# A hybrid encoder block on one core: MLA queries made feature-major, per head pair, with rotary tables turned during the mixer and latents normed for all tokens at once

## Chip, cores and metric

The kernel runs on 1 core of one Trainium2 chip. The metric is the device time of one execution in microseconds (us). The kernel before took 987.62 us, the median of 3 runs (987.09 to 988.03).

## The reference, cut to what matters

One layer on 512 tokens of width 1024: an RMS norm, one input projection that feeds a Mamba-2 (SSD) mixer and a multi-head latent attention (MLA), an output projection of both, a memory cross-attention, a convolution FFN and a last norm. The change touches the MLA queries:

```
q_lat, kv_lat, k_rope = split(u, [384, 640])
q = (rmsnorm(q_lat) @ w_q_up).reshape(b, s, 16, 64 + 32)
q_nope, q_rope = split(q, [64])
kv = (rmsnorm(kv_lat) @ w_kv_up).reshape(b, s, 16, 64 + 64)
q_rope = [t1 * cos - t2 * sin, t1 * sin + t2 * cos]   # t1, t2: halves of 16; k_rope likewise
sc = (q_nope . k_nope + q_rope . k_rope) * 96 ** -0.5, block-causal mask, softmax, times v
```

## The kernel before, in words

Every product runs in three matmuls (`mm3`, L101 to L105): both operands are split into a high and a low part (`split`, L92: a ScalarE copy makes the high part, a VectorE subtraction the low one), and hi*hi, hi*lo and lo*hi add up in one PSUM bank. Weights come as pages of 512 KB over SyncE's DMA queue (`wload`, three raw buffers `wr`), and are split into `wh` and `wl` (four buffers each); while `pool_helps` is set, GpSimd does half of the low part (L158). The PSUM banks are three `acc`, two `tr` (transposes), two `s` (scores), one `pv`.

The order that is written down is a priority: the compiler's list scheduler places each instruction on its engine by a simulated timeline, and fills with later ready work. SyncE and GpSimd issue their DMAs in order.

The mixer walks 16 steps (4 groups of heads by 4 chunks of 128 tokens), each with `ssd_a`, `ssd_b`, `ssd_d` for a chunk. Groups 0 to 2 mix in the projections of the next group; in the last group a string per chunk (`PLAN`, L35) says what goes between: `l` the late units that project the latents (`late_unit`, L665), `i` their setup, `q0` to `q3` and `k0` to `k3` norm and transpose the query and key latents of one 128-token tile (`lat_norm`, L616), `p` a part of the output projection (`out_part`), `U` the query up-projection of heads 0 to 3, `s` and `S` the setup of query and key operands. `lat_norm` takes a sum of squares on ScalarE, a power on GpSimd, a scaling on VectorE, three or two transposes and as many splits into `LT` (the latents feature-major, five tiles of 128 features by 512 tokens).

`q_up` (L712) runs once per four heads: for each of four token tiles nine matmuls of 384 columns (tokens on partitions), a copy to `qrow`, and four GpSimd operations for the rotation. `prep` (L762) then transposes each head's queries back, four 128-token pieces of 96 features, into an `acc` bank, and splits them into one of two operands `qt`. `prep(i + 2)` is called while head i is finished, after the scores of head i + 1. The attention loop (L905) overlaps scores of head i + 1, transposed probabilities and `pv` of head i, and fill units (the rest of the output projection, memory keys and values) at fixed places.

Of the kernel before, what the change touches and what calls it, by code (L numbers as in the profile page):

```python
# [7 lines left out]
F32 = mybir.dt.float32  # L8
# [26 lines left out]
PLAN = ('z z z z d a l l b', 'l l d a i q0 k0 p1 q1 b p1 q2 k1 p1 q3 k2', 'p1 d a k3 p1 b p1', 'p1 d U p2 b p3 s S')  # L35


def shape_constants():
# [4 lines left out]
    m = np.zeros((NT, 2, T), np.float32)  # L43
    for j in range(NT):
        m[j, 0, j * P:j * P + 64] = 1.0
        m[j, 1, j * P + 64:(j + 1) * P] = MASK_NEG
# [16 lines left out]
def tile_block(ctx, tc, x, mem, positions, norm_mix_w, w_in, ssd_conv_w, ssd_conv_b, ssd_dt_bias,  # L63
# [62 lines left out]
    def k4(shape, name, dt=F32):  # L126
        return base.tile(list(shape), dt, name=name, tag="k4", bufs=13)
# [105 lines left out]
    cenT = base.tile([P, NT, SSD_H], F32, name="cenT")  # L233
    acT = dram.tile([NT, SSD_H, P], F32, name="acT")
# [370 lines left out]
    def lat_init():  # L605
# [4 lines left out]
        box["ln"] = qkl[:, QR + KVR:]  # L610
        nc.vector.tensor_scalar(box["qw"], box["qw"], float(QH) ** -0.5, None, ALU.mult)
        x4 = k4([P, 4, 256], "xo")
        xo.extend(x4[:, i] for i in range(3))
        box["lnk"] = [gw[0], x4[:, 3]]

    def lat_norm(t, o, n, w, l0, l1, ln):  # L616
        ss = small([P, 1], "ssl", 2)
        src = lat[:, t, SSD_H + o:SSD_H + o + n]
        nc.scalar.activation(ln, src, AF.Square, accum_out=ss)
        rs = rstd_of(ss, n, "l")  # L620
        nc.vector.scalar_tensor_tensor(ln, src, rs, w, ALU.mult, ALU.mult)
        ps = tr_bank().rearrange("p (k t) -> p k t", k=4)
        for k in range(l0, l1):
            transpose(ps[:, k - l0], ln[:, tsl(k - l0)])
        for k in range(l0, l1):
            split(LT[k][:, 0, tsl(t)], LT[k][:, 1, tsl(t)], ps[:, k - l0])

    def lat_q(t):
        lat_norm(t, 0, QR, box["qw"], 0, 3, box["ln"])

    def lat_kv(t):
        lat_norm(t, QR, KVR, box["kvw"], 3, 5, box["lnk"][t % 2])
        kr = lat[:, t, SSD_H + QR + KVR:]
        tmp = small([P, ROPE], "krt", 1)
        nc.vector.tensor_tensor(tmp[:, 0:H2], kr[:, H2:], sinb[:, t, 0:H2], ALU.mult)
        nc.vector.tensor_tensor(tmp[:, H2:], kr[:, 0:H2], sinb[:, t, H2:], ALU.mult)
        nc.vector.tensor_tensor(kr, kr, cosb[:, t], ALU.mult)
# [589 lines left out]
```

## Time and profile before

| what | before |
|---|---|
| runs shown, median (range) | 987.62 us (987.09 to 988.03) |
| the profiled execution | 987.27 us |
| its span in the profile | 985.5 us |
| its mean granted TensorE clock | 0.994 |
| instructions | 14980 |

The span is the time from the first to the last instruction of the profile; 1.8 us of the profiled execution lie around it. A window row gives, for a stretch of the span, each engine's busy time with its count of instructions, the granted TensorE clock as a share of full speed, and what the DMA engines did. Matmuls are pipelined, so a matmul's own duration is longer than the step from one start to the next; the steps are read from start times.

### The profile page before, as it was taken

What the parts mean: (1) busy time and instruction counts of PE and PEld (TensorE: products, weight loads), DVE (VectorE), ACT (ScalarE), POOL (GpSimd) and SP (SyncE); (2) the same over time, 40 slices, a digit from 0 to 9 for tenths busy, and PEclk for the clock granted to TensorE, in tenths of its full rate; (3) what the DMA queues carried; (4) which work ended last, traced back from release to release, by engine and by line L of the source; (5) the groups of instructions that cost most, each with busy time, mean ns of one, the idle gap of its engine ahead of it and who ended that gap; (6) DMA issues with size and microseconds to landing.
All of it is one profiled execution on the core that took longest, in us unless ns stands there. A gap on an engine that the chain in (4) does not pass through costs nothing.

```text
span 985.5 us, 14980 instructions
## 1 busy us (share of the span) xinstructions
PE 965.7 (98%) x5385; PEld 843.0 (86%) x5385; DVE 662.1 (67%) x1210; ACT 523.4 (53%) x1078; POOL 279.6 (28%) x360
## 2 busy tenths in 40 slices
PE   8999999999999999999999999999999999999997
PEld 6889998898899999988888888888888888888886
DVE  5989999868779786773654435766667666722553
ACT  5677776655477677753544434444444444321442
POOL 2016547656653547452443222000000000000000
PEclk9999999999999999999999999999999999999999
DMA  7653432315423336242241120433223322332462
GB/s 242 208 175 95 116 108 77 97 49 179 155 78 103 113 113 233 86 155 80 86 150 65 65 86 22 128 107 107 86 87 108 105 85 93 113 116 97 156 223 80
DMA packets 90306, 114.07 MB, mean 116 GB/s; under 512 B 5799, under 2 KB 70119, under 8 KB 89848
## 3 DMA queue, kind: packets, MB, share of 16 engines
q1 hardware_dynamic: 88536, 106.78, 34.0%
q0 software_dynamic: 1696, 6.33, 2.1%
q8 instruction: 43, 0.70, 0.3%
q14 instruction: 31, 0.25, 0.1%
HBM read 104.67 MB, written 8.42 MB: 115 GB/s over the span
## 4 chain that ended last, share of the span: by engine, by line
PE 82%; DVE 7%; DMA 3%; ACT 3%; POOL 2%; issue 2%; SPq 0%; POOLq 0%; ACTq 0%; DVEq 0%
PE acc L103 22%; PE acc L105 22%; PE acc L104 22%; PE tr L119 3%; PE s L103 3%; PE s L105 3%; PE s L104 3%; PE pv L811 2%; DMA aE<-acT 2%; DVE wl L157 1%; ACT aE L544 1%; PE acc L119 1%; DVE cu L434 1%; DMA wr<-in_w_in_dram 1%; POOL xdD L550 1%
## 5 line engine op out<-in xcount | busy, mean ns | idle before, releaser
L103 PE MATMUL acc<-Ah,wh 128*128 128x512 f32 (+1 forms) x560 | 215.5, 385 | 0.2 <-ACT Ah L94 0.2
L104 PE MATMUL acc<-Al,wh 128*128 128x512 f32 (+1 forms) x560 | 215.4, 385 | 0.2 <-DVE Al L95 0.2
L105 PE MATMUL acc<-Ah,wl 128*128 128x512 f32 (+1 forms) x560 | 215.0, 384 | 0.0
L95 DVE TENSOR_TENSOR wl<-wr,wh 128x1024 fp32r<-128x1024 f32 (+1 forms) x99 | 120.0, 1213 | 101.6 <-ACT wh L94 100.9
L94 ACT CAST wh<-wr 128x1024 fp32r<-128x1024 f32 (+1 forms) x99 | 102.0, 1031 | 133.5 <-PE acc L104 63.7
L158 POOL TENSOR_TENSOR wl<-wr,wh 128x512 fp32r<-128x512 f32 (+2 forms) x64 | 103.5, 1625 | 86.2 <-ACT wh L156 79.8
L142 POOL TENSOR_TENSOR rs<-ms,neg_half 128x1 f32<-128x1 f32 x18 | 10.8, 600 | 409.5 <-DVE ms L140 397.9
L104 PEld LDWEIGHTS acc<-Al,wh 128*128 128x128 f32 x560 | 105.3, 188 | 20.3 <-DVE Al L95 0.5
L105 PEld LDWEIGHTS acc<-Ah,wl 128*128 128x128 f32 x560 | 105.3, 188 | 20.2
L103 PEld LDWEIGHTS acc<-Ah,wh 128*128 128x128 f32 x560 | 105.2, 188 | 20.0 <-ACT Ah L94 0.5
L156 ACT CAST wh<-wr 128x1024 fp32r<-128x1024 f32 (+2 forms) x64 | 65.4, 1029 | 40.1 <-PE s L105 10.7
L1121 DVE SCALAR_TENSOR_TENSOR cbuf<-acc,fcw,cbuf 128x511 f32<-128x511 f32 (+1 forms) x88 | 65.6, 747 | 26.6 <-ACT cbuf L1119 25.1
L157 DVE TENSOR_TENSOR wl<-wr,wh 128x512 fp32r<-128x512 f32 (+2 forms) x64 | 59.3, 932 | 35.7 <-ACT wh L156 34.7
L103 PE MATMUL acc<-wh,Ah 128*128 128x256 f32 (+2 forms) x240 | 77.2, 323 | 1.0 <-ACT Ah L94 1.0
L105 PE MATMUL acc<-wh,Al 128*128 128x256 f32 (+2 forms) x240 | 76.2, 319 | 0.0
L104 PE MATMUL acc<-wl,Ah 128*128 128x256 f32 (+2 forms) x240 | 75.9, 318 | 0.0
L795 POOL TENSOR_SCALAR p<-p,ri 128x128 f32<-128x128 f32 (+1 forms) x64 | 34.5, 542 | 71.7 <-DVE ri L794 71.1
L103 PEld LDWEIGHTS acc<-wh,Ah 128*128 128x128 f32 x240 | 46.1, 192 | 4.2 <-ACT Ah L94 1.4
L105 PEld LDWEIGHTS acc<-wh,Al 128*128 128x128 f32 x240 | 46.1, 192 | 2.6 <-DVE Al L95 0.3
L104 PEld LDWEIGHTS acc<-wl,Ah 128*128 128x128 f32 x240 | 46.2, 192 | 2.3
L1119 ACT ACTIVATE cbuf<-acc,fcb,fcw 128x512 f32<-128x512 f32 x44 | 34.3, 779 | 24.0 <-PE acc L105 24.0
L104 PE MATMUL acc<-wl,act 128*128 128x512 f32 (+1 forms) x112 | 40.5, 363 | 0.0
(370 smaller groups left out, 2349.3 us busy)
## 6 DMA issues: line engine op xcount, KB each, us to landing
wr<-in_w_ffn_up_dram SPq DMA_DIRECT2D x44, 512.0 KB, 3.5
wr<-in_w_ffn_down_dram SPq DMA_DIRECT2D x33, 512.0 KB, 3.3
wr<-in_w_in_dram SPq DMA_DIRECT2D x26, 512.0 KB, 3.9
wr<-in_w_out_dram SPq DMA_DIRECT2D x16, 512.0 KB, 3.5
aE<-acT POOLq DMA_DIRECT2D x16, 256.0 KB, 3.5
wr<-in_w_mem_k_dram SPq DMA_DIRECT2D x8, 512.0 KB, 4.5
wr<-in_w_mem_v_dram SPq DMA_DIRECT2D x8, 512.0 KB, 3.4
wr<-in_w_mem_q_dram SPq DMA_DIRECT2D x8, 512.0 KB, 3.6
```

The source lines that it names most:

```text
L94: first = nc.scalar.copy(hi, src)
L95: nc.vector.tensor_tensor(lo, src, f32(hi), ALU.subtract)
L103: nc.tensor.matmul(acc, lhsT=lh, rhs=rh, start=first, stop=False)
L104: nc.tensor.matmul(acc, lhsT=lh, rhs=rl, start=False, stop=False)
L105: nc.tensor.matmul(acc, lhsT=ll, rhs=rh, start=False, stop=last)
L119: nc.tensor.transpose(dst, src, ident[:n, :n])
L156: nc.scalar.copy(hi, raw)
L157: nc.vector.tensor_tensor(lo[:, 0:a // 2], raw[:, 0:a // 2], f32(hi[:, 0:a // 2]), ALU.subtract)
L158: nc.gpsimd.tensor_tensor(lo[:, a // 2:], raw[:, a // 2:], f32(hi[:, a // 2:]), ALU.subtract)
L795: nc.gpsimd.tensor_scalar(p_, p_, ri, 1.0, ALU.mult, ALU.mult)
L1119: nc.scalar.activation(u, acc, AF.Identity, scale=fcw[:, 2, m:m + 1], bias=fcb[:, m:m + 1])
L1121: nc.vector.scalar_tensor_tensor(u[:, s:], acc[:, :T - s], fcw[:, 2 - s, m:m + 1], u[:, s:], ALU.mult, ALU.add)
```

## The change

Queries are made with features on partitions; no head is transposed. `q_rope` runs twice (heads 0 to 7, heads 8 to 15): it loads the rotary columns of eight heads, projects the two halves into two banks of 128 rows (8 heads by 16) by 512 tokens, rotates them against tables `csT` whose rows are frequencies, and keeps both halves in `rq`, split. `q_pair` makes the 64 plain features of two heads in one bank, splits them into two of three operands, and copies the heads' rotary rows from `rq` with DMAs on SyncE's queue, two per head. `prep` of an odd head makes the next pair. `rope_tables` builds `csT` after chunk 2 of group 1, with GpSimd copies, eight transposes and two ScalarE copies. `late_unit` takes the sums of squares; `lat_norm` norms all four token tiles with one power; `lat_T` turns one of five feature blocks for all tokens, with one split. The plan string moves accordingly (and has one output part less), the mask rows arrive with their zeros in one DMA per operand, the pool of 4 KB tiles grows from 13 to 14, and the GpSimd DMA scratch is set to 4096 bytes.

```diff
-PLAN = ('z z z z d a l l b', 'l l d a i q0 k0 p1 q1 b p1 q2 k1 p1 q3 k2', 'p1 d a k3 p1 b p1', 'p1 d U p2 b p3 s S')
+PLAN = ('z z z z d a l l b', 'l l d a i n b p1 t0 p1 t1 t2', 'p1 d a t3 p1 t4 b p1', 'p1 d U p2 b p3 s S')
...
+    def lat_norm():
+        rs = small([P, 2 * NT], "lrs", 1)
+        for i, n in enumerate((QR, KVR)):
+            h = slice(i * NT, (i + 1) * NT)
+            nc.vector.tensor_scalar(lss[:, h], lss[:, h], 1.0 / n, EPS, ALU.mult, ALU.add)
+        nc.gpsimd.tensor_tensor(rs, lss, neg_half.broadcast_to([P, 2 * NT]), ALU.pow)
+        for t in range(NT):
+            for i, (o, n, w) in enumerate(((SSD_H, QR, "qw"), (SSD_H + QR, KVR, "kvw"))):
+                v = lat[:, t, o:o + n]
+                nc.vector.scalar_tensor_tensor(v, v, rs[:, i * NT + t:i * NT + t + 1], box[w], ALU.mult, ALU.mult)
...
+    def lat_T(k):
+        ps = tr_bank()
+        for t in range(NT):
+            transpose(ps[:, tsl(t)], lat[:, t, SSD_H + P * k:SSD_H + P * (k + 1)])
+        split(LT[k][:, 0], LT[k][:, 1], ps)
...
+    def rope_tables():
+        for i, tab in enumerate((cosb, sinb)):
+            ps = tr_bank()
+            for t in range(NT):
+                r = small([P, P], "csr", 2)
+                nc.gpsimd.tensor_copy(r.rearrange("p (h c) -> p h c", c=H2),
+                                      tab[:, t, H2:].unsqueeze(1).broadcast_to([P, 8, H2]))
+                transpose(ps[:, tsl(t)], r)
+            nc.scalar.copy(csT[:, i], ps)
...
         nc.scalar.copy(lat[:, t, 256:], acc)
+        for i, (o, m) in enumerate(((SSD_H, QR), (SSD_H + QR, KVR))):
+            nc.scalar.activation(acc[:, 0:m], lat[:, t, o:o + m], AF.Square, accum_out=lss[:, i * NT + t:i * NT + t + 1])
...
-    def q_up(q4):
...
+    def q_rope(g):
+        raw = base.tile([P, 3, 8, ROPE], F32, name="wr", tag="wr", bufs=3)
+        for k in range(3):
+            nc.sync.dma_start(raw[:, k], mla_w_q_up[0][tsl(k), :].rearrange("p (h c) -> p h c", h=MLA_H)[
+                :, 8 * g:8 * g + 8, NOPE:])
...
+        for k in range(3):
+            hv, lv = (a[:, k].rearrange("p s h c -> p h s c") for a in (hi, lo))
+            split(hv, lv, raw[:, k].rearrange("p h (s c) -> p h s c", s=2))
+        acc = []
+        for s in range(2):
+            acc.append(acc_bank())
             for k in range(3):
+                w = [a[:, k, s].rearrange("p h c -> p (h c)") for a in (hi, lo)]
+                mm3(acc[s], w, (LT[k][:, 0], LT[k][:, 1]), k == 0, k == 2)
+        for s in range(2):
+            a, b = f32(rq[s][:, 0]), f32(rq[s][:, 1])
+            nc.vector.tensor_tensor(b, acc[s], csT[:, 0], ALU.mult)
+            nc.vector.tensor_tensor(a, acc[1 - s], csT[:, 1], ALU.mult)
+            nc.gpsimd.tensor_tensor(b, b, a, ALU.add if s else ALU.subtract)
+            nc.scalar.copy(rq[s][:, 0], b)
+            nc.vector.tensor_tensor(rq[s][:, 1], b, f32(rq[s][:, 0]), ALU.subtract)
+
+    def q_pair(pr):
+        raw = base.tile([P, 3, 2, NOPE], F32, name="wr", tag="wr", bufs=3)
+        for k in range(3):
+            nc.sync.dma_start(raw[:, k], mla_w_q_up[0][tsl(k), :].rearrange("p (h c) -> p h c", h=MLA_H)[
+                :, 2 * pr:2 * pr + 2, 0:NOPE])
...
+        split(hi, lo, raw.rearrange("p k h c -> p k (h c)"))
+        acc = acc_bank()
+        for k in range(3):
+            mm3(acc, (hi[:, k], lo[:, k]), (LT[k][:, 0], LT[k][:, 1]), k == 0, k == 2)
+        for e in range(2):
+            q = qts[(2 * pr + e) % 3]
+            split(q[0:NOPE, 0], q[0:NOPE, 1], acc[e * NOPE:(e + 1) * NOPE])
+            r = H2 * (2 * pr % 8 + e)
+            for s in range(2):
+                nc.sync.dma_start(f32(q[NOPE + H2 * s:NOPE + H2 * (s + 1)]), f32(rq[s][r:r + H2]))
...
-        ps = acc_bank()
-        for t in range(NT):
-            transpose(ps[0:QH, tsl(t)], st["q"][t][:, h % 4])
-        split(qts[h % 2][0:QH, 0], qts[h % 2][0:QH, 1], ps[0:QH])
+        elif h + 1 < MLA_H:
+            q_pair((h + 1) // 2)
...
+            if (g, c) == (1, 2):
+                rope_tables()
...
+    q_pair(0)
     prep(0)
...
-        if i % 4 == 1 and i + 3 < MLA_H:
-            q_up((i + 3) // 4)
+        if i == 3:
+            q_rope(1)
```

## Rows read from the trace of the kernel before

**Rows 1.** The page: busy time of each engine, share, instructions

```profile
PE 965.7 (98%) x5385; PEld 843.0 (86%) x5385; DVE 662.1 (67%) x1210; ACT 523.4 (53%) x1078; POOL 279.6 (28%) x360
```

**Rows 2.** Windows: stretch, busy PE, PEld, DVE, ACT, POOL, clock, DMA

```profile
120.00:145.00 25.00, 25.00 (x162) 22.54 (x161) 23.16 (x44) 17.96 (x40) 11.56 (x16) 1.00 0.33 90
...
200.00:270.00 70.00, 65.07 (x422) 61.00 (x421) 54.62 (x137) 37.60 (x102) 43.46 (x61) 0.95 0.42 133
...
270.00:440.00 170.00, 169.89 (x1187) 160.05 (x1186) 134.78 (x319) 124.15 (x314) 86.83 (x132) 1.00 0.39 125
```

**Rows 3.** Windows of the mixer's last steps

```profile
216.00:220.00 4.00, 3.43 (x20) 3.15 (x18) 1.49 (x7) 2.26 (x5) 3.17 (x5) 1.00 0.00 0
220.00:224.00 4.00, 2.97 (x21) 2.57 (x21) 3.61 (x4) 2.47 (x5) 3.83 (x3) 1.00 0.15 49
224.00:228.00 4.00, 3.49 (x22) 3.29 (x23) 4.00 (x14) 2.69 (x8) 2.52 (x3) 0.81 0.63 205
228.00:232.00 4.00, 4.00 (x29) 4.00 (x29) 3.85 (x11) 0.92 (x4) 0.62 (x1) 0.76 0.86 274
...
244.00:248.00 4.00, 2.40 (x9) 1.20 (x8) 1.68 (x7) 2.23 (x11) 4.00 (x8) 1.00 0.52 162
248.00:252.00 4.00, 3.03 (x17) 2.81 (x17) 3.41 (x10) 1.05 (x4) 3.92 (x10) 0.80 0.15 50
252.00:256.00 4.00, 4.00 (x27) 4.00 (x27) 2.95 (x9) 1.78 (x4) 2.85 (x5) 0.78 0.14 39
```

**Rows 4.** Timeline there: start, us, instruction, idle before and its releaser

```profile
224.33 0.39 PE L103 MATMUL s<-xs,Br 128*128 128x256 f32 x1 [1.15 <-DVE cbm L541]
...
247.64 0.62 DVE L621 SCALAR_TENSOR_TENSOR qkl<-lat,rsl,qkl 128x384 f32<-128x384 f32 x1 [2.17 <-POOL rsl L142]
...
248.97 0.55 PE L119 MATMUL tr<-cst,qkl 128*128 128x128 f32 x3 [2.08 <-DVE lt L95]
```

**Rows 5.** The tile qrow: ns min/median/max, first and last start

```profile
L119 PE MATMUL acc<-cst,qrow x64: 270/272/280, 261.8 to 421.2; 128*96 128x128 f32 x64
...
L728 POOL TENSOR_TENSOR qrow<-qrow,cosb x16: 454/463/907, 245.5 to 379.8; 128x128 f32<-128x128 f32 x16
```

**Rows 6.** Timeline of PE: steps of transposes and matmuls

```profile
238.52 0.34 PE L103 MATMUL acc<-wh,lt 128*128 128x384 f32 x1
...
239.91 0.33 PE L105 MATMUL acc<-wh,lt 128*128 128x384 f32 x1
...
268.72 0.60 PE L119 MATMUL acc<-cst,qrow 128*96 128x128 f32 x4
...
269.27 0.28 PE L104 MATMUL acc<-wl,Bh 128*128 128x256 f32 x1
269.39 0.28 PE L105 MATMUL acc<-wh,Bl 128*128 128x256 f32 x1
...
271.58 0.40 PE L103 MATMUL s<-kt,qt 100*128 100x512 f32 x1
...
272.05 0.39 PE L105 MATMUL s<-kt,qt 100*128 100x512 f32 x1
```

**Rows 7.** The tile kt

```profile
L95 DVE TENSOR_TENSOR kt<-acc,kt x16: 669/688/694, 264.1 to 413.4; 64x512 fp32r<-64x512 f32 x16
```

**Rows 8.** The tiles lt and qkl: splits and scalings of the latents

```profile
L95 DVE TENSOR_TENSOR lt<-tr,lt x20: 273/277/292, 226.8 to 260.4; 128x128 fp32r<-128x128 f32 x20
...
L621 DVE SCALAR_TENSOR_TENSOR qkl<-lat,rsl,qkl x4: 603/612/620, 212.7 to 247.6; 128x384 f32<-128x384 f32 x4
L621 DVE SCALAR_TENSOR_TENSOR gw<-lat,rsl,qkl x2: 478/478/479, 213.3 to 248.2; 128x256 f32<-128x256 f32 x2
```

**Rows 9.** DMA: SyncE's queue, and the issue with the shortest runs

```profile
q1 hardware_dynamic: 88536, 106.78, 34.0%
...
rot<-in_positions_dram SPq DMA_DIRECT2D x1, 2.0 KB, 2.1
```

**Rows 10.** Timeline of POOL in the middle of the mixer

```profile
145.25 1.12 POOL L567 TENSOR_TENSOR xdD<-xdD,y 128x256 f32<-128x256 f32 x1 [7.83 <-DVE msy L140]
```

More of the change, by code (lines that the diff above doesn't have):

```diff
@@ L609, in lat_init @@
         box["qw"], box["kvw"] = row_tile(qkl[:, 0:QR], mla_q_norm_w), row_tile(qkl[:, QR:QR + KVR], mla_kv_norm_w)
-        box["ln"] = qkl[:, QR + KVR:]
         nc.vector.tensor_scalar(box["qw"], box["qw"], float(QH) ** -0.5, None, ALU.mult)
         x4 = k4([P, 4, 256], "xo")
[L613 to L637, printed above, removed]
-        nc.vector.tensor_tensor(kr, kr, tmp, ALU.add)
+        xo.extend(x4[:, i] for i in range(4))
@@ new lines, in tile_block @@
+    lss = small([P, 2 * NT], "lss", 1)
+    def lat_norm():
[8 more added lines that the diff above has]
+                nc.vector.scalar_tensor_tensor(v, v, rs[:, i * NT + t:i * NT + t + 1], box[w], ALU.mult, ALU.mult)
+        kr = lat[:, :, SSD_H + QR + KVR:]
+        tmp = small([P, P], "csr", 2).rearrange("p (t c) -> p t c", t=NT)
+        nc.vector.tensor_tensor(tmp[:, :, 0:H2], kr[:, :, H2:], sinb[:, :, 0:H2], ALU.mult)
+        nc.vector.tensor_tensor(tmp[:, :, H2:], kr[:, :, 0:H2], sinb[:, :, H2:], ALU.mult)
+        nc.vector.tensor_tensor(kr, kr, cosb, ALU.mult)
+        nc.vector.tensor_tensor(kr, kr, tmp, ALU.add)
@@ L680, in tile_block @@
     yM = act_pair("A")
-    qrow = [k4([P, 2, 4, QH], "qrow") for _ in range(2)]
+    rq = [k4([P, 2, T], "rq", F32R) for _ in range(2)]
     kts, qts = [], []
     def setup_kq1():
-        for b in range(2):
-            kt = k4([P, 2, T], f"kt{b}", F32R)
-            qt = k4([P, 2, T], f"qt{b}", F32R)
-            for i, (tl, w) in enumerate(((qt, masks[:, 0]), (kt, masks[:, 1]))):
-                nc.vector.memset(f32(tl[QH:KROWS, 1]), 0.0)
-                nc.gpsimd.dma_start(tl[QH:KROWS, 0], w)
-            kts.append(kt)
-            qts.append(qt)
+        for b in range(5):
+            tl = k4([P, 2, T], f"qk{b}", F32R)
+            nc.gpsimd.dma_start(tl[QH:KROWS], masks[:, b % 2])
+            (kts if b % 2 else qts).append(tl)
     def setup_kq2():
@@ L702, in tile_block @@
     st = {}
-    rts = [k1([P, 4, ROPE], "rt") for _ in range(2)]
     wkh, wkl = (page(n).rearrange("p i (n c) -> p i n c", n=2) for n in ("wkh", "wkl"))
@@ L766, in prep @@
             k_pair(h % 4 // 2)
-        ps = acc_bank()
-        for t in range(NT):
-            transpose(ps[0:QH, tsl(t)], st["q"][t][:, h % 4])
-        split(qts[h % 2][0:QH, 0], qts[h % 2][0:QH, 1], ps[0:QH])
+        elif h + 1 < MLA_H:
+            q_pair((h + 1) // 2)
     POFF = (384, None, 0, 512)
     def scores(h, qi):
-        q, k = qts[h % 2], kts[h % 2]
+        q, k = qts[h % 3], kts[h % 2]
         n = P * (qi + 1)
@@ L859, in do @@
         elif op == "U":
-            q_up(0)
+            q_rope(0)
         elif op == "S":
```

39 lines of the change are left out of this document (14 added, 25 removed).

## Prediction

> **What bounds the kernel now.** I read the page first: TensorE has work 98% of the span, VectorE 67%, ScalarE 53%, GpSimd 28% [rows 1]. So time goes only where TensorE loses work, idle time or half-clock time. The windows by stretch come next [rows 2]. From 270 to 440 us, the attention loop, TensorE is busy 169.89 of 170 us at granted clock 1.00: there every matmul taken out is a matmul's step off the end, as long as the others keep up (VectorE 134.78 of 170 us, 79%). From 200 to 270 us, the last mixer group, it is busy 65.07 of 70 us, at a mean clock of 0.95: 4.9 us idle, and some time at the lower of the two levels (1.2 GHz, the higher is 2.4). The windows of 4 us [rows 3] put this into two holes. The first: 0.57, 1.03 and 0.51 us idle from 216 to 228 us (2.1 us), then granted clocks of 0.81 and 0.76, a loss of 0.19 and 0.24 times 4 us (1.7 us). The second: 1.60 and 0.97 us idle from 244 to 252 us (2.6 us), then 0.80 and 0.78 (1.7 us). Together 8.1 us. Who held TensorE stands in the timeline [rows 4]: in the first hole a 1.15 us wait for VectorE's mask product of the mixer; in the second a 2.08 us wait for VectorE's split of the latents, behind a scaling that itself had waited 2.17 us for GpSimd's power.
>
> **The change, part by part.** The sum is made against the profiled execution, 987.27 us; the median of the runs shown is 0.35 us above it.
>
> **Transposes taken out.** `prep` turns 16 heads back, 64 transposes [rows 5]. Their cost is their step, not their 272 ns: from the start of a group of four at 268.72 to the second matmul behind it at 269.27 are 0.55 us, and such a matmul alone steps 0.12 (269.27 to 269.39) [rows 6]. So a group costs 0.43 us, and 16 of them 6.9 us. All lie at 261 to 421 us, almost all in the full stretch. Minus 6.9.
>
> **Matmuls of the query projection.** Before 4 x 4 x 9 = 144 of 384 columns, after 2 x 18 + 8 x 9 = 108 of 512: the same 55,296 columns. Eight steps of 384 columns take 1.39 us (238.52 to 239.91), 0.174 each; two steps of 512 take 0.47 (271.58 to 272.05), 0.235 each [rows 6]. 144 x 0.174 = 25.1, 108 x 0.235 = 25.4. Plus 0.3.
>
> **Rotary tables.** Eight new transposes at 0.43/4 us in a full stretch (25.00 of 25 us [rows 2]): plus 0.9. Their eight GpSimd copies have no row; the nearest, a 128x128 GpSimd product, takes 0.463 [rows 5], so 3.7 us at most in GpSimd's queue, ahead of the next decay load that GpSimd issues. GpSimd stands idle 7.83 us right before 145.25 us [rows 10], which hides them; uncovered they cost up to 3.7. I take 0, the idle row being the nearer one. The two ScalarE copies lie in ScalarE's idle 7 of those 25 us [rows 2].
>
> **Latents.** Before: 20 splits of 128 columns, 0.277 us of VectorE each [rows 8], 5.5 us, in eight rounds of sum, power, scaling, transpose; after: 5 splits of 512 columns at about 0.69 (the split of 512 columns of `kt` [rows 7]), 3.4 us, and one round. The transposes stay 20. What moves is when: nothing can be scaled before the fourth late unit is evacuated and squared, and then 4 x 0.612 + 4 x 0.478 = 4.4 us of scalings [rows 8] come at once, near 224 us, where VectorE is full (3.61, 4.00 and 3.85 of 4 us [rows 3]). Queued behind that burst are the mixer's mask product and the splits of the output weights, and TensorE waits for both. So the second hole should go (minus 4.3), and the first should deepen, by between 0 and 4.4 us plus a further low-clock time like its own 1.7. I take a third of that, 2.0, as TensorE then has two output parts of 12 matmuls to run (2 x 12 x 0.12 = 2.9 us). Net minus 2.3; ends minus 8.1 (both holes gone) and plus 6.1 (the burst in full, the second hole kept). Squares move into the late unit's `acc` bank, which is held about 1 us longer; two other banks cover it, and without them it is inside the upper end.
>
> **Rotation.** 16 evacuations and 64 GpSimd operations go. Each `q_rope` has six VectorE operations of 512 columns, at 0.69 [rows 7] 4.1 us, and three small splits, at most 2.1. One lies in the mixer's tail, where the saved splits and 8 small rescalings pay for most of it, and one in attention. There the seven `q_pair` weight splits add at most 7 x 0.69 = 4.8; the head splits are as many and as long as before. So VectorE has at most 134.8 + 6.2 + 4.8 = 145.8 us in about 163 us, 89%. I cost it at 0: what hides it is TensorE's own work; if it doesn't hide, it is a rival below.
>
> **Copies of rotary rows.** 32 new DMAs of 64 KB on SyncE's queue, each behind the split of `rq` and the last scores that read the operand. A small DMA lands in 2.1 us [rows 9]. With three operands a pair has a whole head (about 10 us of attention) before its scores, so 0; uncovered it would be 2.1 per pair. Weight loads stand behind them in the same queue; three raw pages are ahead. The mask loads lose four VectorE fills and keep to GpSimd: 0. The smaller DMA scratch serves GpSimd's few DMAs and the larger pool only frees waits: 0; neither shows in the trace. The output part that moves into the loop is the same work later: 0.
>
> **Short runs.** The rotary columns are loaded in runs of 128 bytes, 3,072 of them for each `q_rope`, and the plain ones in 256 bytes. No row has such a load. On SyncE's queue 88,536 packets took 34.0% of 16 engines' 985.5 us, 3.8 ns per packet when all 16 share [rows 9], so 3,072 of them 11.7 us; the 512 runs of 4 bytes of the positions landed in 2.1 us in all, at most 4.1 ns each, so 12.6. Below, a run costs nothing of its own. I take 11.7 us of transfer, ahead of need, as DMA is busy 0.42 and 0.39 of these stretches [rows 2]: 0 on the path. The Trainium skill, page "DMA: Bandwidth & Descriptors", section Specifications, speaks against this part: runs under 512 bytes don't reach the line rate. Its section Bandwidth has about 10.5 ns per packet, an estimate of 32 us per load. By that the loads would outlast their lead and the sum would end above the time before; the row on the positions, below 4.1 ns, speaks against such a price.
>
> **Sum.** -6.9 + 0.3 + 0.9 - 2.3 = -8.0, so 979.3 for the profiled execution and 979.6 as a median.
>
> **The rivals.**
> First, **both holes go** and nothing deepens: -6.9 + 0.3 + 0.9 - 8.1 = -13.8, 973.5. For it: less work on VectorE and GpSimd in the tail. Against: the first hole was not made by the latents [rows 4].
> Second, **VectorE becomes the bound of attention**: at 89% with bursts of 4 us, the transposes' gain is eaten and only the tail's and the tables' terms stay: 0.3 + 0.9 - 2.3 = -1.1, 986.2 to 986.5. For it: a step of the loop has no idle anywhere. Against: a chain of idle TensorE would have to appear where there is 0.1 us in 170 [rows 2].
> Third, **the burst of scalings starves the tail**: the upper end of the latents, -6.9 + 0.3 + 0.9 + 6.1 = +0.4, 987.7 to 988.0, no change. Against: GpSimd's eight powers, which made the second hole, are one.
> Fourth, on the other side, **the short loads hold the weights up**: a `q_rope` load stands 11.7 us in the rings in front of the output weights. TensorE then lives on pages already split: three parts of 12 matmuls, 4.3 us. 7.4 us are open, twice 14.8: -8.0 + 14.8 = +6.8, 994.1. It decides from 4 us open per load, where the gain is used up. The page named above is this rule; by its per-packet price the open time would be an estimate of 28 us per load. For it: 0.63 and 0.86 of the DMA engines are busy at 224 to 232 us [rows 3], when such a load could run. Against: this load replaces one that could be asked for as early, and the tail's other windows are emptier.
>
> **How the numbers follow.** My chances: the forecast 0.54, both holes 0.12, VectorE 0.13, the burst 0.09, the short loads 0.12. The predicted time is the forecast's, 979.6. A measurement can tell 0.2%, 2.0 us, from no change, so faster is below 985.6 and slower above 989.6. Forecast and both holes are faster (0.66), of VectorE's case about half and of the burst's a quarter, by their own spread: 0.74. The rest of VectorE's and most of the burst's give 0.10 within 0.2%. The short loads and a little of the two give 0.16 slower. The range goes from 972.5, below the case of both holes, to 988.5, above the burst's; it leaves out the short loads (0.12) and the edges (0.08).
>
> **What would show it.** Right: no matmuls that read `qrow`; some 4 to 8 us less of TensorE busy time between the first scores and the last `pv`, at clock 1.00; no idle of TensorE behind the latents' splits before the first scores; idle still there near 216 to 228 us, now behind VectorE's scalings. Wrong: idle inside attention whose releaser is VectorE, or a DMA into the query operands or `wr`; a loss in the middle of the mixer behind the decay loads; low clocks lasting longer than the four windows of before.

## The result, and the profile after

The changed kernel takes 1004.96 us (median of 4 runs) against 987.83 for the kernel before, timed beside it: a ratio of 1.0176, 95% interval 1.0153 to 1.0199, 17.1 us slower. The forecast was 979.6, faster, and the range ended at 988.5. The profiled execution takes 1003.79 us, with a span of 1001.7.

The page's first line, busy time of each engine, answers to [rows 1]:

```profile
PE 966.9 (97%) x5293; PEld 834.8 (83%) x5293; DVE 670.3 (67%) x1191; ACT 522.0 (52%) x1059; POOL 252.5 (25%) x298
```

TensorE has 92 instructions less and yet as much busy time. Where the span grew stands in the windows (us, busy PE, PEld, DVE, ACT, POOL, granted clock, DMA share, GB/s), first the stretches of [rows 2], then three that cut the same time into the mixer's tail, the heads, and the place where the memory keys begin:

```profile
200.00:270.00 70.00, 59.75 (x359) 54.92 (x358) 50.76 (x96) 33.60 (x80) 32.60 (x37) 0.93 0.38 106
270.00:440.00 170.00, 160.49 (x1078) 144.74 (x1077) 135.98 (x325) 117.66 (x298) 60.56 (x80) 0.99 0.47 137
```

```profile
200.00:280.00 80.00, 67.56 (x410) 62.00 (x409) 57.95 (x111) 37.80 (x90) 34.04 (x39) 0.94 0.42 114
280.00:360.00 80.00, 76.27 (x498) 67.63 (x496) 67.65 (x162) 57.11 (x148) 24.56 (x35) 1.00 0.41 112
360.00:400.00 40.00, 36.57 (x234) 32.24 (x235) 33.57 (x83) 28.46 (x73) 15.08 (x22) 0.96 0.51 150
```

The kernel before, in the same three stretches:

```profile
200.00:280.00 80.00, 75.07 (x495) 70.55 (x494) 63.19 (x160) 44.54 (x122) 47.21 (x66) 0.96 0.41 130
280.00:360.00 80.00, 79.91 (x567) 75.91 (x566) 65.72 (x166) 60.50 (x161) 38.65 (x70) 1.00 0.31 96
360.00:400.00 40.00, 39.98 (x292) 38.38 (x291) 30.84 (x68) 29.91 (x71) 26.50 (x38) 1.00 0.59 196
```

TensorE's idle time, width less busy, goes from 4.9 to 12.4 us in the tail, from 0.1 to 3.7 in the heads and from 0.0 to 3.4 in the last stretch: 14.6 us more. Time at the lower clock, width times what the granted clock lacks to 1.00, goes from 3.2 to 4.8 in the tail and from 0 to 1.6 in the last stretch: 3.2 more. The heads, where a matmul less was to be a step off the end, now have holes.

Who held TensorE, by the view of its waits between 200 and 470 us (total, times, longest):

```profile
PE acc L103 <- DVE lat L660: 3.9, 2, 2.4
PE acc L103 <- DVE xo L660: 2.2, 1, 2.2
PE s L103 <- DVE cbm L542: 1.7, 1, 1.7
PE s L103 <- ACT S L94: 1.7, 1, 1.7
PE s L103 <- ACT p L823: 1.6, 3, 0.7
PE acc L103 <- DVE v L784: 1.1, 1, 1.1
PE tr L119 <- DVE lt L95: 1.1, 1, 1.1
PE acc L103 <- DMA memT<-memT_d: 1.1, 1, 1.1
```

Most of it is VectorE, and mostly VectorE is late with something else than the latents: with the sum of an output part (L660) or the mask product (L542). Its timeline in the first hole shows the burst of scalings, 4.4 us by forecast and 3.77 measured, and something that was not forecast: two rescalings of 4 columns that take 0.70 and 1.26 us.

```profile
227.38 0.70 DVE L622 TENSOR_SCALAR lss<-lss 128x4 f32<-128x4 f32 x1
...
228.20 1.26 DVE L622 TENSOR_SCALAR lss<-lss 128x4 f32<-128x4 f32 x1
...
233.04 3.77 DVE L627 SCALAR_TENSOR_TENSOR lat<-lat,lrs,qkl 128x384 f32<-128x384 f32 x8
```

In the second hole a pass that usually takes 0.69 us takes 4.24, as long as GpSimd runs three passes of its own (timeline of both engines):

```profile
256.46 1.30 POOL L158 TENSOR_TENSOR wl<-wr,wh 128x512 fp32r<-128x512 f32 x1
256.52 4.24 DVE L157 TENSOR_TENSOR wl<-wr,wh 128x512 fp32r<-128x512 f32 x1
257.70 2.51 POOL L743 TENSOR_TENSOR rq<-rq 128x512 f32<-128x512 f32 x2
```

This is called a hold below. `L158` is GpSimd's half of a weight's low part, `L157` VectorE's half of the same tile; the two are released together.

The third place is the memory keys' operand `memT`. `mem_k` reloads it into the buffer that held the mixer's output, so it can be asked for only behind the last output part. In the kernel before the reload has a cover:

```profile
365.71 1.21 POOL L827 DMA_DIRECT2D memT<-memT_d  x2 [3.78 <-PE s L784]
```

```profile
366.28 0.42 PE L103 MATMUL acc<-wh,lt 128*128 128x384 f32 x1
...
375.45 0.34 PE L105 MATMUL acc<-wh,lt 128*128 128x384 f32 x1
...
375.85 0.36 PE L103 MATMUL acc<-memT,wh 128*128 128x256 f32 x1
```

The 36 matmuls of the last `q_up` stand there, and TensorE is busy all through. The changed kernel has no such block; its reload is asked for at 384.18 us, and TensorE lives on the heads' chain of scores, exponential, scaling and transposes until it lands:

```profile
384.18 1.19 POOL L858 DMA_DIRECT2D memT<-memT_d  x2
...
388.77 0.55 PE L119 MATMUL tr<-cst,p 128*128 128x128 f32 x3 [0.91 <-POOL p L826]
...
392.00 0.58 PE L103 MATMUL acc<-memT,wh 128*128 128x256 f32 x1 [1.09 <-DMA memT<-memT_d]
```

### The profile page after: what moved, and what is told of

It reads as the page before. It is cut to its first block, busy times and chain, and to the rows that moved or that the text cites. A ratio compares the mean times of both kernels' runs of the same rounds, so it can differ in the third digit from the quotient of the medians.

```text
span 1001.7 us, 14779 instructions
## 1 busy us (share of the span) xinstructions
PE 966.9 (97%) x5293; PEld 834.8 (83%) x5293; DVE 670.3 (67%) x1191; ACT 522.0 (52%) x1059; POOL 252.5 (25%) x298
## 4 chain that ended last, share of the span: by engine, by line
PE 79%; DVE 10%; DMA 4%; ACT 3%; issue 3%; POOL 1%; SPq 0%; POOLq 0%; DVEq 0%; ACTq 0%
PE acc L103 22%; PE acc L104 21%; PE acc L105 21%; PE tr L119 3%; PE s L103 3%; PE s L104 2%; PE s L105 2%; PE pv L842 1%; DMA aE<-acT 1%; DVE wl L157 1%; DMA memT<-memT_d 1%; DVE cu L435 1%; DVE wl L95 1%; DVE aE L547 1%; PE pv L584 1%
## 5 line engine op out<-in xcount | busy, mean ns | idle before, releaser
L95 DVE TENSOR_TENSOR wl<-wr,wh 128x1024 fp32r<-128x1024 f32 (+2 forms) x109 | 124.6, 1147 | 104.4 <-ACT wh L94 103.9
L94 ACT CAST wh<-wr 128x1024 fp32r<-128x1024 f32 (+2 forms) x109 | 106.0, 977 | 140.7 <-PE acc L104 67.0
L158 POOL TENSOR_TENSOR wl<-wr,wh 128x512 fp32r<-128x512 f32 (+1 forms) x60 | 96.6, 1616 | 84.8 <-ACT wh L156 81.1
L157 DVE TENSOR_TENSOR wl<-wr,wh 128x512 fp32r<-128x512 f32 (+1 forms) x60 | 58.0, 971 | 42.7 <-ACT wh L156 42.4
L156 ACT CAST wh<-wr 128x1024 fp32r<-128x1024 f32 (+1 forms) x60 | 62.2, 1040 | 37.5 <-PE acc L104 14.1
L103 PE MATMUL acc<-wh,Bh 128*128 128x256 f32 x128 | 38.2, 298 | 6.1 <-DVE lat L660 3.9
```

Source lines behind the costliest of these rows:

```text
L94: first = nc.scalar.copy(hi, src)
L95: nc.vector.tensor_tensor(lo, src, f32(hi), ALU.subtract)
L103: nc.tensor.matmul(acc, lhsT=lh, rhs=rh, start=first, stop=False)
L156: nc.scalar.copy(hi, raw)
L157: nc.vector.tensor_tensor(lo[:, 0:a // 2], raw[:, 0:a // 2], f32(hi[:, 0:a // 2]), ALU.subtract)
L158: nc.gpsimd.tensor_tensor(lo[:, a // 2:], raw[:, a // 2:], f32(hi[:, a // 2:]), ALU.subtract)
```

## The experiments

All were timed beside the kernel before; "+" is against its median there, and the ratio has its 95% interval. After the first six, a table gives the stretches of all.

**1. Only the pool and the scratch.** The kernel before with two sizes of the change.

```diff
-tag="k4", bufs=13)
+tag="k4", bufs=14)
-num_devices=1)
+num_devices=1, dynamic_dma_scratch_size=4096)
```

> The kernel before with only the larger pool (14 tiles of 4 KB) and the smaller GpSimd DMA scratch (4096 bytes). Both theories below, latents and queries, put this at the time before, 986 to 990 us, with the attention stretch as full as before. If the buffers or the scratch themselves made the loss, it is above 995 us.

987.17 us, +0.3, ratio 1.0003 (0.9993 to 1.0012). The sizes cost nothing, as forecast.

**2. The queries alone.** The changed kernel with `lat_q`, `lat_kv` and the written order of before.

```diff
-PLAN = (..., 'l l d a i n b p1 t0 p1 t1 t2', 'p1 d a t3 p1 t4 b p1', ...)
+PLAN = (..., 'l l d a i q0 k0 p1 q1 b p1 q2 k1 p1 q3 k2', 'p1 d a k3 p1 b p1', ...)
```

> The changed kernel with the latents normed per token tile again, and the plan string of before; the queries stay feature-major. Theory latents (the batch of scalings on VectorE makes the tail's loss, 11.1 us of idle and low clock at 220 to 248 us): 994 us or less, and the later holes shrink with it. Theory queries (GpSimd's rotation holds VectorE, the row copies come late, attention has less work that waits for nothing): 1000 us or more, with the holes at 256 to 276 and 312 to 396 us still there.

996.85 us, +10.0, ratio 1.0102 (1.0079 to 1.0125): between the two ranges, so it decides for neither theory.

**3. The latents alone.** The kernel before with `lat_norm`, `lat_T` and the changed order.

```diff
-PLAN = (..., 'l l d a i q0 k0 p1 q1 b p1 q2 k1 p1 q3 k2', 'p1 d a k3 p1 b p1', ...)
+PLAN = (..., 'l l d a i n b p1 t0 p1 t1 t2', 'p1 d a t3 p1 t4 b p1', ...)
```

> The kernel before with the batch norm of the latents and the new plan string alone, token-major queries kept. Theory latents: 995 us or more, with the hole at 224 to 248 us. Theory queries: 983 to 990 us, with a full attention stretch.

1006.6 us, +19.7, ratio 1.0203 (1.0188 to 1.0218). Both halves lose, and by 29.7 together where the change loses 17.1: they share a loss.

**4. The combination on VectorE.** In `q_rope` of the changed kernel:

```diff
-            nc.gpsimd.tensor_tensor(b, b, a, ALU.add if s else ALU.subtract)
+            nc.vector.tensor_tensor(b, b, a, ALU.add if s else ALU.subtract)
```

> The changed kernel with the rotation's add and subtract (four operations of 128x512, 1.29 us each on GpSimd) on VectorE. In the changed kernel's trace VectorE's split of a weight page took 4.24 us where 0.69 is usual, just while GpSimd ran three long operations from 256.5 to 260.2 us. Theory of the shared access (GpSimd's long operations hold VectorE's two-operand ones): the 4.24 us operation is gone, 998 us or less. Rival (VectorE is only late because it is full): 1002 to 1008 us, since the work has moved onto it.

1001.18 us, +14.3, ratio 1.0152 (1.0127 to 1.0177). The time lies between theory and rival, and its interval overlaps that of the change, so as a gain it is no more than a tendency. But the hold is shortened: the same pass now takes 1.78 us, beside the one GpSimd pass that is left, and the first scores come at 266 us instead of 274.

```profile
254.80 1.29 POOL L158 TENSOR_TENSOR wl<-wr,wh 128x512 fp32r<-128x512 f32 x1
254.86 1.78 DVE L157 TENSOR_TENSOR wl<-wr,wh 128x512 fp32r<-128x512 f32 x1
```

**5. The moved part alone.** The prediction costed at 0 that the changed order has one output part less in the mixer. The kernel before with that alone:

```diff
-'l l d a i q0 k0 p1 q1 b p1 q2 k1 p1 q3 k2'
+'l l d a i q0 k0 p1 q1 b q2 k1 p1 q3 k2'
```

> The kernel before with one output part taken out of the mixer's written order, so that it becomes a unit of the attention loop; nothing else changes. Theory: the reload of the memory operand, which can start only when the last output part has read its buffer, comes one slot later, behind the 36 matmuls of the last query block instead of under them; TensorE then waits some 6 to 9 us for the reload, first memory-key matmul about 9 us after its issue with idle time before it: 993 to 996. Rival (as the prediction costed it, the same work later): 987, within 1 us, and no idle time of over 1 us at the first memory-key matmul.

1000.6 us, +14.3, ratio 1.0141 (1.0123 to 1.0159): nearly the loss of the whole change, from one step that computes the same. Its windows around the reload:

```profile
380.00:384.00 4.00, 1.92 (x8) 0.96 (x6) 4.00 (x6) 2.99 (x9) 3.98 (x6) 1.00 0.93 315
384.00:388.00 4.00, 0.48 (x4) 0.51 (x4) 4.00 (x7) 0.67 (x2) 2.02 (x3) 0.64 1.03 382
388.00:392.00 4.00, 3.33 (x12) 2.39 (x11) 1.54 (x4) 1.27 (x3) 2.50 (x5) 0.50 1.00 359
392.00:396.00 4.00, 4.00 (x17) 3.28 (x18) 1.03 (x3) 1.45 (x4) 0.00 (x0) 0.58 0.07 24
```

6.3 us idle, and then 4 us windows at 0.64, 0.50 and 0.58, the lower of the two clocks: 5.1 us more. But the timeline shows a mechanism that the theory did not have:

```profile
381.89 1.21 POOL L827 DMA_DIRECT2D memT<-memT_d  x2
382.21 4.37 DVE L157 TENSOR_TENSOR wl<-wr,wh 128x512 fp32r<-128x512 f32 x1
383.11 1.29 POOL L158 TENSOR_TENSOR wl<-wr,wh 128x512 fp32r<-128x512 f32 x1
384.35 0.46 POOL L728 TENSOR_TENSOR qrow<-qrow,cosb 128x128 f32<-128x128 f32 x1
384.76 1.26 POOL L158 TENSOR_TENSOR wl<-wr,wh 128x512 fp32r<-128x512 f32 x1
...
387.52 1.09 PE L119 MATMUL tr<-cst,p 128*128 128x128 f32 x4 [3.52 <-DVE PT L95]
```

The reload's issue falls among the GpSimd rotations of the last `q_up`; GpSimd's passes pile up behind it, and a VectorE pass is held for 4.37 us. TensorE waits 3.52 us for VectorE, not for the transfer.

**6. The latents with the part kept.** Run 3 with a third `p1`.

```diff
-'l l d a i n b p1 t0 p1 t1 t2'
+'l l d a i n b p1 t0 p1 t1 p1 t2'
```

> The kernel before with the latents normed for all tokens at once, as in the run with the latents alone, but with the third output part left in that piece of the mixer's order, so the attention loop has the parts it had. Theory of two separate losses: the reload lies under the last query block again and the 6 us of idle time at 380 to 400 us go, the holes at 220 to 280 us stay: 998 to 1001. Rival, that the attention's loss is all a consequence of the later start and of the scratch order in it: 1005 to 1007, as with the part moved.

994.29 us, +8.0, ratio 1.0080 (1.0064 to 1.0095), less than either expected. The part is worth 11.7 of the latents' 19.7 us. At 360 to 400 us, without it (run 3) and with it:

```profile
360.00:400.00 40.00, 33.77 (x207) 30.40 (x206) 29.45 (x61) 24.27 (x60) 20.84 (x34) 0.87 0.55 191
```

```profile
360.00:400.00 40.00, 40.00 (x294) 38.59 (x293) 30.80 (x70) 29.20 (x71) 22.76 (x36) 1.00 0.58 198
```

From the same windows of every run, TensorE's idle us and the clock (1.00 where none stands):

```
                                   against before   200-280      280-360   360-400
before                                    -          4.9 0.96      0.1       0.0
change                                  +17.1       12.4 0.94      3.7       3.4 0.96
2  queries alone                        +10.0        9.1 0.94      2.9       3.3 0.96
3  latents alone                        +19.7        8.0 0.91      1.1       6.2 0.87
4  combination on VectorE               +14.3        9.9 0.94      4.1       2.0 0.96
5  part moved alone                     +14.3        5.9 0.98      1.9       6.3 0.87
6  latents, part kept                    +8.0       10.1 0.96      1.4       0.0
7  empty unit before the keys           +16.8       12.6 0.94      3.7       2.6 0.96
8  no scalings                          +13.6       10.1 0.96      4.2       3.0 0.91
9  part moved, two keys without halves  +13.3        5.9 0.98      2.2       6.2 0.87
10 part moved, four keys without        +12.5        6.1           2.4       3.4 0.91
11 transposes put back                  +19.1       10.2 0.91      2.3 0.98  2.7 0.96
12 change without GpSimd halves         +11.1        5.0 0.98      4.0       5.4 0.91
13 before without GpSimd halves          -2.1        1.7 0.98      1.1       0.0
14 change, part kept                    +12.3       10.4 0.94      1.9       4.0 0.91
15 queries, reload a unit ahead          +9.3        7.7 0.94      4.9       2.7 0.96
16 as 15, no halves, two units ahead     +8.9        6.6 0.94      4.5       1.5
17 queries, first rotation left out      +8.8        7.9 0.96      4.2       3.0 0.91
18 change, mended                        -1.1        2.9           3.5       1.5
```

The last stretch is full in before, 6 and 13 (in run 1 too), the kernels that have the last `q_up` behind the reload, and in no other.

**7. An empty unit before the memory keys,** in the changed kernel.

```diff
-fills = ... for i in range(16)] + [lambda m=m: mem_k(m) ...
+fills = ... for i in range(16)] + [lambda: None] + [lambda m=m: mem_k(m) ...
```

> The changed kernel with one empty unit between the last output part and the first memory key, so that the reload is issued where the memory keys used to begin and the keys come a slot later. Theory: that the keys wait for the reload costs 4 to 5 us; since the reload is issued only by the first key's unit in program order but waits on the buffer alone, it starts no earlier in the queue's order unless the queue runs ahead; if it runs ahead the wait goes (1000 to 1001), if the issue moves with the unit the wait stays (1005). Rival: the attention's loss there is not the reload: 1005 with TensorE idle elsewhere.

1003.08 us, +16.8, ratio 1.0178 (1.0151 to 1.0206). No change: the reload is issued by the first key's own unit, at 382.96 us, and moved with it. It tells that the queue does not run ahead, and no more.

**8. Without the scalings,** in `lat_norm` of the changed kernel.

```diff
-        for t in range(NT):
-            for i, (o, n, w) in enumerate(((SSD_H, QR, "qw"), (SSD_H + QR, KVR, "kvw"))):
-                v = lat[:, t, o:o + n]
-                nc.vector.scalar_tensor_tensor(v, v, rs[:, i * NT + t:i * NT + t + 1], box[w], ALU.mult, ALU.mult)
```

> The changed kernel without the eight scalings of the latents by root and weight (left out: the norm's scaling of both latents; the squares, the power and the rotation of the key part stay). Theory: VectorE's burst of 3.8 us is what the transposes of the latents wait for, so the idle time at 220 to 248 us shrinks by 3 to 4 us and the time to 1000.5 to 1002. Rival: the burst is only one link, what comes late is the late units and squares ahead of it, and VectorE is full there anyway: 1004 to 1005.

999.84 us, +13.6, ratio 1.0134 (1.0118 to 1.0151): 3.5 us less, the burst's own 3.77 to within the intervals. The hold of 4.24 us is gone here too (the longest pass of `L157` takes 1.78), so the 3.5 us are not the burst's alone. It is one link of the tail's loss; the tail keeps 10.1 us of idle time.

**9 and 10. The hold in run 5.** On top of run 5's edit, the first two, then the first four memory keys' weights split without GpSimd:

```diff
         if m % 2 == 0:
+            pool_helps[0] = m > 0
             mem["p"] = wcols(w_mem_k[0], P * m, 256)
+            pool_helps[0] = True
```

> The kernel with the one output part moved (1000.6 us), with the weights of the first two memory keys split by VectorE alone instead of half by GpSimd. Theory: the loss is a VectorE pass of 0.69 us that was held for 4.37 us beside a train of GpSimd passes at 382 us, and the scores, the transposes and the clock behind it; without GpSimd's halves in that train no pass there takes over 1.8 us, TensorE's idle time at 384 to 388 us and the low clock behind it go, 989 to 993. Rival: the reload of the memory operand is what TensorE waits for there, and the time stays at 998 to 1001.

1000.83 us, +13.3, ratio 1.0129 (1.0114 to 1.0145). The hold did not go, it took another pass, beside the next page's halves:

```profile
381.43 3.72 DVE L95 TENSOR_TENSOR Al<-yt,Ah 128x512 fp32r<-128x512 f32 x1
...
382.12 2.48 POOL L158 TENSOR_TENSOR wl<-wr,wh 128x512 fp32r<-128x512 f32 x2
```

So the second, with `m > 3` in the place of `m > 0`:

> The kernel with the one output part moved (1000.6 us), with the weights of the first four memory keys split by VectorE alone. The run with two keys left a hold of 3.72 us on another pass, beside GpSimd's two halves of the next page. Theory: with no half left in that stretch GpSimd's train is only the rotation and the two loads, no VectorE pass is held for over 1.8 us, and TensorE's 6 us of idle time at 380 to 400 us and the low clock behind it go: 988 to 993. Rival: the units after the moved part wait for the reload itself or for the chain of scores: 997 to 1001.

999.41 us, +12.5, ratio 1.0128 (1.0111 to 1.0145). Now the hold is gone, and the stretch's idle time and clock loss go from 6.3 and 5.2 to 3.4 and 3.6 us. But the time does not follow beyond its interval, and the rival's range holds it: without the cover TensorE has only the heads' chain (waits of 1.73, 1.35 and 0.31 us for scores, exponential and the reload), and the clock falls behind that too.

**11. The transposes put back** into the changed kernel, of a constant, read by nobody:

```diff
+        ps = acc_bank()
+        for t in range(NT):
+            transpose(ps[0:QH, tsl(t)], cst[:, P:P + QH])
```

> The changed kernel with four transposes of a constant put back into every head's preparation, as many and as long as the query transposes that the change removed, with nobody reading their result. Theory: behind the change the heads are no longer paced by TensorE's work but by the chain of scores, exponential, scaling and split, so the transposes fill idle time and cost less than 2 us: 1004 to 1007. Rival, that TensorE's work still sets the pace: 64 transposes at 0.107 us come on top, 1011 to 1012.

1006.56 us, +19.1, ratio 1.0192 (1.0176 to 1.0209). 64 transposes cost 2.0 us in the changed kernel, by the two intervals not told apart from nothing; 6.9 would be a ratio of 1.0246, outside the interval. Its heads, for comparison with the 76.27 above:

```profile
280.00:360.00 80.00, 77.75 (x509) 70.15 (x509) 66.25 (x160) 55.64 (x146) 24.19 (x36) 0.98 0.39 110
```

The heads are 1.5 us busier than in the change in the same 80 us: part of the transposes lie in holes.

**12 and 13. No GpSimd halves** from the mixer's last steps on, in the changed kernel and in the kernel before:

```diff
-    pool_helps[0] = i > 9
+    pool_helps[0] = False
```

> The changed kernel with every weight split on VectorE alone from the tail of the mixer on (GpSimd's halves of the low parts left to VectorE). Theory: held VectorE passes (one of 4.24 us at 256 us, several of 1.5 to 1.8) are a large part of the loss; without them 996 to 1000, though VectorE does more. Rival: VectorE's own load is what makes the heads late, and 0.7 us more for each half brings 1007 to 1012.

998.56 us, +11.1, ratio 1.0112 (1.0080 to 1.0144): some 6 us less than the change, as the theory had it. The tail's idle time falls from 12.4 to 5.0 us, although VectorE got the work of both halves. The reload's hole grows.

```profile
200.00:280.00 80.00, 75.00 (x497) 70.59 (x496) 60.62 (x133) 44.96 (x111) 26.58 (x36) 0.98 0.49 131
...
360.00:400.00 40.00, 34.60 (x227) 31.15 (x226) 26.89 (x63) 24.58 (x60) 7.97 (x15) 0.91 0.53 154
```

> The kernel before with every weight split on VectorE alone from the tail of the mixer on. Theory: before has no hold over 1.8 us, and VectorE has room, so the halves are worth little either way: 985 to 989. Rival: VectorE's load makes the heads late, 990 to 996.

984.90 us, -2.1, ratio 0.9978 (0.9968 to 0.9987), a little faster than expected and faster than both kernels. In the tail the halves cost the kernel before something as well:

```profile
200.00:280.00 80.00, 78.29 (x544) 74.50 (x542) 67.13 (x175) 49.88 (x135) 38.09 (x63) 0.98 0.43 137
```

Later they pay. At 480 to 520 us, around the last of the memory values, the kernel before is full, and run 13 has 1.8 us of idle time and a lower clock:

```profile
480.00:520.00 40.00, 40.00 (x200) 33.56 (x199) 25.81 (x42) 20.46 (x38) 18.70 (x15) 1.00 0.42 131
```

```profile
480.00:520.00 40.00, 38.24 (x174) 31.16 (x173) 21.98 (x34) 15.54 (x30) 1.48 (x3) 0.96 0.36 118
```

The four kernels without halves (12, 13, 16, 18) all have this hole, of 1.8 to 1.9 us. Halves off in the tail and on behind the heads was not run.

**14. The change with the part kept,** by the line of run 6:

```diff
-'l l d a i n b p1 t0 p1 t1 t2'
+'l l d a i n b p1 t0 p1 t1 p1 t2'
```

> The changed kernel with the third output part left in its place in the mixer's order. Theory: in the change the late query block and its GpSimd passes are gone, so the moved part makes no hold at the reload there and the reload is uncovered with or without it; the latents with the part kept (+8.0) and the queries alone (+10.0) add up: 1003 to 1006. Rival: the moved part costs the change what it costs the latents alone (12.3 us): 991 to 995.

999.23 us, +12.3, ratio 1.0121 (1.0106 to 1.0136). Neither: the part costs the change some 5 us, less than the 11.7 it costs the latents alone, and not nothing. The reload's hole stays, now with a wait of 3.2 us for the transfer itself. The hold of 4.24 us is gone (longest pass of `L157` 1.78), so what the part costs by itself in the change is not separated from it.

**15 and 16. The queries mended.** Run 2 with the combination on VectorE and the reload issued by a unit of its own, one ahead of the first key; then two ahead and without halves:

```diff
-fills = ... + [lambda m=m: mem_k(m) for m in range(8)]
+fills = ... + [mem_load] + [lambda m=m: mem_k(m) for m in range(8)]
```

> The new queries with the latents and the order of before (996.9 us), the rotation's combination on VectorE instead of GpSimd, and the memory operand's reload issued one unit ahead of the first memory key. Theory: the reload's wait of 3.3 us and the low clock behind it go (about 5) and the combination gives 2 to 4 as in the changed kernel: 988 to 991, level with before at best since the transposes' 6.9 us fall into the chain of the heads. Rival: both are made up for by other waits of the heads, 994 to 998.

996.83 us, +9.3, ratio 1.0096 (1.0077 to 1.0114): the rival. The reload is issued at 373.1 us, and the first key still waits 2.7 us for it at 379.6; one unit ahead is too little.

> The new queries with the latents and the order of before, the rotation's combination on VectorE, no GpSimd halves, and the reload issued two units ahead of the first memory key (996.8 us with the halves and one unit). Theory: the holds of 1.4 to 1.8 us and the reload's wait of 2.7 us with the low clock behind it go: 989 to 992, still not under before since the heads run at the pace of their chain. Rival: 995 to 998, the loss is the tail's chain of the latents, which neither touches.

995.85 us, +8.9, ratio 1.0088 (1.0061 to 1.0115): the rival again. The reload's clock loss goes, the tail's loss stays (6.6 us idle at 0.94). The longest wait, 2.5 us, is for a split of the latents, which are as before. What keeps the new queries with the old latents some 9 us above before stays open.

**17. The first rotation left out** of run 2, to price VectorE's part in that tail:

```diff
         for s in range(2):
+            if g == 0:
+                split(rq[s][:, 0], rq[s][:, 1], acc[s])
+                continue
```

> The queries alone (996.9 us) with the rotation of the first eight heads left out: two splits of the projection in the place of six VectorE products and differences and two GpSimd combinations, so that those heads' rotary rows are unrotated. Theory: the tail's 14 us of idle and slow time, 6 more than before, come from VectorE, on which the query block now works where TensorE and GpSimd did before; with the work out of it the first scores come 4 to 6 us earlier and the time is 991 to 993, and what is left above before (4 to 6) is the attention loop's. Rival: the tail waits for the latents' chain whatever the rotation does: 995 to 997.

996.00 us, +8.8, ratio 1.0077 (1.0061 to 1.0094): the rival. The tail waits for the same step of the latents (4.1 us behind L140 in both), with or without the rotation.

**18. The change mended:** the edits of runs 14, 4 and 12, and the reload two units ahead.

```diff
-fills = ... + [lambda m=m: mem_k(m) for m in range(8)]
+fills = ... + [mem_load, lambda: None] + [lambda m=m: mem_k(m) for m in range(8)]
```

> The changed kernel with the third output part in its old place, the combination on VectorE, no GpSimd halves, and the reload issued two units ahead of the first memory key. Theory: these mend 12 to 15 of the 18 us (5.7 for the part, 6.4 for the halves with the holds, and up to 3.8 for the combination as far as it isn't the same hold), the rest is VectorE's load in the tail and the chain of the heads: 990 to 994. Rival: the losses overlap and it stays at 995 to 998; or they add up with the reload's and it is level with before, 985 to 989.

986.12 us, -1.1, ratio 0.9990 (0.9981 to 1.0000): level with before, which is the second rival; the theory of 990 to 994 failed. The tail has less idle time than before and no low clock; the heads keep their holes.

```profile
200.00:280.00 80.00, 77.10 (x525) 72.79 (x524) 64.73 (x145) 48.81 (x122) 27.22 (x38) 1.00 0.53 145
280.00:360.00 80.00, 76.50 (x510) 68.94 (x509) 70.88 (x171) 57.97 (x153) 18.65 (x32) 1.00 0.36 100
360.00:400.00 40.00, 38.47 (x267) 35.13 (x266) 33.35 (x77) 29.82 (x76) 8.96 (x17) 1.00 0.64 214
```

So the loss of the changed kernel is not in what it computes but in how its pieces fall beside each other: four edits of order and engine, none of which takes work away, bring back 18 us. Three of them were also run alone (14, 4 and 12: 4.9, 2.8 and 6.1 us, together 13.8). The reload two units ahead was not, so whether the rest is its own or comes of the four together stays open. What is left of its gain is then nothing: run 13, without the change, is at 0.9978.

## Why the prediction was wrong, by its steps

**"The output part that moves into the loop is the same work later: 0."** By the price of a single line this step failed worst. It asked what the part costs and not what stands behind it in its row: the last part frees the buffer that the memory operand is reloaded into. One unit later the reload misses the 36 matmuls that covered it. Alone it measured +14.3 (run 5), between runs 3 and 6 11.7, in the change about 5 (run 14), probably since there the cover is gone anyway. In 20 kernels the stretch is full only with the cover; asking two units ahead (runs 16 and 18) leaves 1.5 us of idle time without it. How the 14.3 divides between the hold, the chain and what comes later stays open, as run 10 removed the hold and gained no more than its interval.

**"Transposes taken out: minus 6.9."** The size was right, the place was not: a step off the end "as long as the others keep up". They don't: TensorE's idle time in the heads goes from 0.1 to 3.7 us, and run 11 puts the same number back for 2.0 us. The forecast read 169.89 of 170 as a bound that stays one when its work shrinks; that the transposes were cover between the links of a chain fits both, but the kernel before without them was not run. That this gain is eaten was the second rival's claim, but not by its mechanism: VectorE, put at up to 145.8 us there, measured 135.98 of 170, about what it was before.

**"Latents: minus 2.3."** Wrong in sign: +8.0 with the part kept (run 6). The burst was sized well (4.4 against 3.77) and costs at most some 3.5 (run 8, where the hold goes with it), between the 2.0 that was taken and the upper end of 6.1. The second hole did not go: it moved to where VectorE is held beside GpSimd. What the step left out is that VectorE's passes get longer there, not more: without the halves the tail's idle time is 5.0 instead of 12.4 us (run 12).

**"Rotation: 0."** VectorE's work for the first eight heads is indeed near 0 (run 17 gains 1.2 within the intervals). The two GpSimd combinations were not looked at as neighbours of VectorE: they are two of the three passes in the hold of 4.24 us. Without them the hold shrinks to 1.78 us (run 4), for 2.8 us of time, not beyond its interval.

**Right** was that the tables do no harm: TensorE's busy time in the first 200 us is 192.35 us in the change and 192.54 before. Their 0.9 is too small to be read from one pass: the mixer's same pass (`aE`, 1.6 us) starts at 203.33 to 203.99 us in seven kernels without the tables and at 202.90 to 204.70 in nine with them. Right were the pool and scratch (run 1), and the short loads, which are no bottleneck. By the view of DMA issues (KB each, median us to landing):

```profile
qk<-rq SPq DMA_DIRECT2D x32, 64.0 KB, 3.2
...
wr<-in_mla_w_q_up_dram SPq DMA_DIRECT2D x6, 128.0 KB, 2.8
```

A load of 1,024 runs of 128 bytes lands in 2.8 us, so the three of a `q_rope` in 8.4 even one after the other: below the 11.7 us taken. The Trainium skill's price per packet ("DMA: Bandwidth & Descriptors", section Bandwidth, measured there on loads that GpSimd issues), by which I estimated 32 us, does not fit this trace. The row copies land in 3.2 us; in the change nobody waits for one, but the first scores do in runs 2 (1.6 us) and 14 (2.1).

**The sum.** The 17.8 us more of idle and slow time, less some 6 of work taken out, leave about 4 of the 16.2 us between the two spans unexplained. The steps from one matmul's start to the next close it. Against the median step of each shape in the kernel before (0.227 us for 512 columns, 0.120 for 256, 0.109 for a transpose) all steps together run over by 26.7 us before and by 49.5 in the change. That is 22.8 more: 8.7 in the tail, 6.9 in the heads, 6.4 in the last stretch and 0.7 elsewhere. The work, counted in the same steps and with the tables, falls by 6.8, and 22.8 less 6.8 is 16.0. Idle time shows less than that in part because a matmul counts as busy to its own end, past its step, so a hole costs more than its idle time. By the same count run 18 runs over by 4.1 us in the tail, against 11.3 before, and by 6.5 in the heads, against 0.7: there the transposes' 6.9 stay eaten.

## What to carry to other kernels

Before a unit is moved in a hand-written order, look at what is released by the last of its kind, a reload above all, and at what covers that now; a full TensorE may owe its fullness to such a block. Where TensorE is full but fed by a chain of other engines, the busy share doesn't tell what taking work out gains: time the kernel with the work simply left out before you build the change. And where GpSimd shares elementwise work with VectorE, judge the pair together and stretch by stretch, since a train of GpSimd passes can stop VectorE for its whole length, while elsewhere the help is needed.

## What the runs showed of the hardware

VectorE's and GpSimd's subtractions over whole tiles in SBUF exclude each other, and who starts first goes first. In the kernel before, both halves of a weight are released by the same copy, VectorE starts 0.04 us earlier, and GpSimd pays:

```profile
254.17 0.69 DVE L157 TENSOR_TENSOR wl<-wr,wh 128x512 fp32r<-128x512 f32 x1 [0.51 <-ACT wh L156]
254.21 1.79 POOL L158 TENSOR_TENSOR wl<-wr,wh 128x512 fp32r<-128x512 f32 x1 [1.13 <-ACT wh L156]
```

When GpSimd is first, its pass takes 1.30 and VectorE's is held, and not for one GpSimd pass but for the train of them: 4.24 us beside three in the change, 4.57 beside five in run 3, 4.37 in run 5, and 1.78 beside one in run 4. In run 5 the held pass starts while GpSimd issues the reload (381.89 to 383.10 us), so the issue belongs to the train. In the kernel before the longest of the 64 passes of `L157` takes 1.77. The Trainium skill, page "SBUF — State Buffer", section "SBUF: two separate sides", has the rule of an exclusive lock that the first to start keeps for its whole instruction. These passes agree with that, and show more: through back-to-back GpSimd instructions VectorE stays held from one to the next. Not every GpSimd pass does this: beside its power of 8 columns (229.54 to 231.57 us in the change) VectorE's sum at 230.31 and its split at 230.84, both over two operands in SBUF, took 0.28 and 0.68 us, as they do in run 12 with GpSimd idle.

Passes of four columns are held too: the second of VectorE's rescalings took 1.26 us beside a weight's half, the first 0.70 beside a GpSimd product, and with GpSimd free one takes 0.16 (runs 3 and 6). GpSimd's power of 8 columns took 2.03 us in eight kernels and 2.23 in two, with and without halves beside it, where one of 1 column takes about 0.55: that is its own price.
